# Decoder trunk with windowed attention: second key tile's rotation ahead of the second maxima, its split one pass later, early output weights' splits behind the second maxima

## The chip, the cores and the metric

The kernel runs as one program on one core of a Trainium2 chip. The metric is the device time of one execution in microseconds (us). All times inside the profiled execution are counted from the start of its span.

## The reference

The program is a two-layer decoder trunk in float32 for 512 tokens of width 1024: a gated short convolution with a SwiGLU layer, then sliding-window attention with sinks on shared keys and values, with another SwiGLU layer. The change touches only the attention, of which this is the core:

```python
k_sh = partial_rotary(k_sh.reshape(bsz, s, N_KV_HEADS, HEAD_DIM), cos, sin)
q = partial_rotary(q, cos, sin)
attn = sliding_window_sink_attention(q, k_sh, v_sh, b_sinks[j]) @ b_w_o[j]
# in sliding_window_sink_attention, 16 query heads on 4 key heads, blocks of 128, window 128:
scores = jnp.einsum('bnqhgd,bnkhd->bnhgqk', qb, kk).astype(jnp.float32) * scale
scores = jnp.where(valid[None, :, None, None], scores, NEG)
probs = jax.nn.softmax(jnp.concatenate([scores, sink], axis=-1), axis=-1)[..., :-1]
out = jnp.einsum('bnhgqk,bnkhd->bnqhgd', probs.astype(v.dtype), vv)
```

## The kernel before

Every float32 matrix operand is split into a high part (ACT copies it to a narrower type) and a low part (an elementwise engine subtracts), and each product is three matmuls: high by low, high by high, low by high. So for each operand there is an ACT instruction and a subtraction on DVE or POOL.

The attention runs in ten passes over eight pairs of heads, in the loop at the end of the kernel. Pass i works on several pairs at once: scores, maxima, exponents and scaling of pair i; transposition and the product with the values (`weigh`) of pair i-1; projection, rotation and split of the queries of later pairs. Each engine carries out its instructions in program order, and that order is written by hand in the string `ORDER` (line 47), one token a step, in which the digit is the half or the quarter of the step and a trailing `-` means one pair earlier. The tokens that matter here:

- `S0`, `S1`: `scores` (L1306, PE) of the two halves, into the two banks called psc. Both halves use the same two banks, so S1 waits until the maxima of the first half have read them, and S0 of the next pass waits for the maxima of the second half.
- `M0`, `M1`: `maxima` (L1318, DVE): four instructions, each adds the mask, scales and takes the row minimum of the negated scores. `E..`: `exponents` on ACT (L1334, L1341). `N0`, `N1`: `normalise` on DVE: a sum `se` (L1346), a reciprocal (L1348) and four scalings `s` (L1351).
- `T0` to `T3`: `turn` (L1363, PE): transposes the scaled exponents of the pass before. `P`, `L`: the split of what was transposed, `phi` on ACT (L1376) and `plo` on DVE (L1380; `lp` for the last block). `W0` to `W3`: `weigh`, the matmuls called po. `O-`: the split of po (L1400 ACT, L1401 DVE).
- `Q0` to `Q3`: projection of the queries (pq, L192 to L194, PE). `R-`: their rotation, `rope`: a shuffle (L1244) and a product with the cosines (L1246) on DVE, then a product with the sines (L1247) and a sum (L1248) on POOL. `H-`: `rope_split`: `rhl` on ACT (L1253) and on POOL (L1254).
- `K`: the same `rope` and `rope_split` for the second of two key tiles, in pass 2 alone. Its operand is the bank pk[1]; its results, `rhi` and `rlo`, are first read by S0 of pass 4. The first key tile was rotated before the loop.
- `G`: the split of query weights, `whi` on ACT (L187) and `wlo` on DVE (L188). `g0`, `g1`: the same for four tiles of the output weights ("early", used by `Z0`, `Z1` from pass 5 on), which happens in passes 4 and 6 (L187, L188 in pass 4, two half tiles by L181, L182 in pass 6). Their loads are issued by SP in the order of the program, through a ring of seven buffers.

POOL's queue also issues transfers that sum blocks of weights for the second SwiGLU layer in memory (`issue`, L546, tiles hsum), some behind each `R-` and each `H-`.

Of the kernel before, what the change touches and what calls it, by code (L numbers as in the profile page):

```python
# [44 lines left out]

EARLY_IN, REST_IN = 2, 0
ORDER = (
    "R- S0 T0 g0 T1 O- Q0 M0 Q1 Z0 P0 P1 S1 T2 T3 L0 Q2 L1 G M1 E00 E01 H- Q3 P2 P3 E10 E11 Z1 z0 K W0 L2 L3 A A A N0 W1 W2 N1 W3 g1 z1"
)
STEP = {  # L50
    "S": "scores", "M": "maxima", "E": "exponents", "N": "normalise", "T": "turn", "P": "high",
# [22 lines left out]
def yoco_kernel(  # L74
# [22 lines left out]
    nc = tc.nc  # L97
# [19 lines left out]
    def slot(s, dt=F32, w=S):  # L117
        return big.tile([P, w], dt, tag="slot", name=name(s), padded_shape=[P, S])
# [4 lines left out]
    def halves(s, dt=F32):  # L123
        w = wide(s, dt)
        return w[:, :S], w[:, S:]
# [3 lines left out]
    def bank(s, pool=None):  # L129

        if pool is None:
            pool = (ps_mm, ps_sc, ps_mm, ps_pt)[turn[0] % 4]
            turn[0] += 1
        return pool.tile([P, S], F32, tag="bank", name=name(s))
# [39 lines left out]
    def split_weights(src, raw=None, slots=False):  # L174
        if raw is None:
            raw = fetch(src)
        if slots:
            hi, lo = Two("whi", F32R), Two("wlo", F32R)
            for h in range(2):
                c = slice(h * S, (h + 1) * S)  # L180
                nc.scalar.activation(hi[:, c], raw[:, c], AF.Copy)  # L181
                nc.vector.tensor_tensor(out=lo[:, c], in0=raw[:, c], in1=hi[:, c].bitcast(F32),  # L182
                                        op=ALU.subtract)
            return hi, lo
        hi = wsp.tile([P, D], F32R, tag="whi", name=name("whi"))
        lo = wsp.tile([P, D], F32R, tag="wlo", name=name("wlo"))
        nc.scalar.activation(hi, raw, AF.Copy)  # L187
        nc.vector.tensor_tensor(out=lo, in0=raw, in1=hi.bitcast(F32), op=ALU.subtract)  # L188
        return hi, lo
# [347 lines left out]
    def issue(n, behind=None):  # L537

        for dst, src, op in issues[:n]:
            if len(dst.shape) == 3:  # L540
                dst, src = (t.rearrange("k (a b) c -> (k a) (b c)", b=4) for t in (dst, src))
            else:
                dst, src = (t.rearrange("(a b) c -> a (b c)", b=2) for t in (dst, src))
            kw = {} if op is None else {"accum_op": op}
            made = tc.keep_in_program_order(
                nc.gpsimd.dma_start(dst, src, max_dma_last_dim=4 * 4 * S, **kw))  # L546
            if behind is not None:
                tc.add_manual_dep(
                    made.ins, behind.ins.name, mybir.DependencyInfo(
                        mybir.DependencyClass.Sync, mybir.DependencyReason.DATA),  # L550
                    reason="pace")
        del issues[:n]
# [3 lines left out]
    for l in range(2):  # L556
# [3 lines left out]
        for rd, (f0, f1) in enumerate(ROUNDS[:-1]):  # L560
            k = slice(f0 // 2, f1 // 2)
# [4 lines left out]
    def sum_on(at):  # L566

        issue(len(issues))
        if at in BEGIN:
            summing.append(sums_of[BEGIN[at]])  # L570
        for x in summing:
            x.step()
        summing[:] = [x for x in summing if x.steps]
# [295 lines left out]
    def close(ws, x, k0, res, ahead, then=None, each=2):  # L869


        n = len(x) - k0

        def part(ps, t, half, ks):
            unit(ps, t, ws[len(ws) // 2 * half :], x, ks, n, k0)

        begun = [bank("pmix", ps_mm) for _ in range(2)]
        for half in range(2):
            part(begun[half], 0, half, range(n - 1))
            for _ in range(each if half == 0 or each > 1 else 0):  # L880
                ahead.one()
        for t in range(NB):
            for half in range(2):
                if t == 0:
                    ps = begun[half]
                    part(ps, t, half, range(n - 1, n))
                else:
                    ps = bank("pmix", ps_mm)
                    if (t, half) == (NB - 1, 1):
                        part(ps, t, half, range(2))  # L890
                        for b in range(4):
                            res.turn(b, (0, 1))
                        part(ps, t, half, range(2, n))
                        for f in range(4):
                            res.split(0, f, 0)
                        res.square_mix(t, 0)
                        res.square(NB - 2)
                        res.scale(t, 0)
                    else:
                        part(ps, t, half, range(n))  # L900
                res.take(t, half, ps)
                if (t, half) != (NB - 1, 0):
                    res.square_mix(t, half)
            if t < NB - 1:
                tile_done(res, t, square=t < NB - 2)
            if t == 0 and then:
                then()
# [40 lines left out]
    def first_weights(l):  # L948
        return ([w_gu[l, f, j] for f in range(2) for j in range(2)]
                + [w_gb[l, 0, b] for b in range(2)])  # L950
# [274 lines left out]
    pk = [bank("pk", ps_mm) for _ in range(2)]  # L1225
# [16 lines left out]
    def rope(ps, eng):  # L1242
        sh = slot("sh")
        nc.vector.stream_shuffle(sh, ps, swap)  # L1244
        a = slot("ra")
        nc.vector.tensor_tensor(out=a, in0=ps, in1=ctab, op=ALU.mult)  # L1246
        eng.tensor_tensor(out=sh, in0=sh, in1=stab, op=ALU.mult)  # L1247
        eng.tensor_tensor(out=a, in0=a, in1=sh, op=ALU.add)  # L1248
        return a

    def rope_split(a, eng, large=False):
        hi, lo = halves("rhl", F32R) if large else (slot("rhi", F32R), slot("rlo", F32R))
        nc.scalar.activation(hi, a, AF.Copy)  # L1253
        eng.tensor_tensor(out=lo, in0=a, in1=hi.bitcast(F32), op=ALU.subtract)  # L1254
        return hi, lo
# [172 lines left out]
    with tc.manual_schedule(engines=ALL):  # L1428
        last_tile(res, [[(0, 4)], [(0, 5)], [], [(0, 6), (0, 7), (1, 0), (1, 1)],
                        [(1, f) for f in (4, 5, 2, 3, 6, 7)]])  # L1430
        for hf in range(2):
            c = slice(hf * 256, (hf + 1) * 256)
# [32 lines left out]
        ks = [rope_split(rope(pk[0], nc.vector), nc.vector)]  # L1465
# [15 lines left out]
    with tc.manual_schedule(engines=ALL):  # L1481
        sum_on("a0")
        for i in range(KT + 2):
            if i == KT:
                res = Update(mix_o, B_ATT, [G_FPRE[1]])
                res.leaves = True
                ahead = Ahead(first_weights(1))
            if i == KT + 1:
                res.load()
            for c in ORDER.split():  # L1490
                if c == "A":
                    if i == KT:
                        ahead.one()
                    continue
                if c == "K":
                    if i == 2:
                        ks.append(rope_split(rope(pk[1], nc.gpsimd), nc.gpsimd))
                    continue
                late = c.endswith("-")
                op, n = c[0], [int(d) for d in c[1:].rstrip("-")]  # L1500
                t = i - late
                if op == "g":

                    u = 2 * (t - EARLY - 1) + n[0]
                    if u in (-2, -1, 2, 3):
                        j = u + 2 if u < 0 else u
                        early_w.append(split_weights(w_o[j // 2, j % 2], slots=j >= EARLY_IN))
                    continue
                if op in "SMENTPLWO":
                    t -= op in "TPLWO"  # L1510
                    of = hp
                elif op in "QRH":
                    t += LEAD
                    of = qs
                elif op == "G":
                    t += LEAD + 1
                    of = qs
                    if KT <= t < KT + 4:
                        j = t - KT
                        rest_w.append(split_weights(w_o[j // 2, 2 + j % 2], slots=j >= REST_IN))  # L1520
                else:
                    t = 2 * (t - EARLY - 1) + n.pop(0)
                    of = early
                if 0 <= t < len(of) and not (op in "RH" and t < LEAD - 1):
                    getattr(of[t], STEP[op])(*n)
                if op in "RH" and i <= KT:
                    issue(len(issues) // 2 if op == "R" else len(issues))
            if i <= KT:
                sum_on(f"a{i + 1}")
        close(rest_w, at, EARLY, res, ahead, lambda: sum_on(f"a{KT + 2}"), 1)  # L1530
# [96 lines left out]
```

## Time and profile before

| | |
|---|---|
| runs shown | 1022.95, 1023.82, 1023.06 us (median 1023.06) |
| the profiled execution | 1023.55 us |
| its span, first to last instruction | 1021.8 us |
| mean granted TensorE clock | 0.998 |
| the ten passes of the attention | about 549 to 655 us of the span |

A row of the timeline gives the start, the duration, the engine, the line of the kernel, the operation, output and inputs, shapes and, where the engine sat idle before it, how long and what ended that (in brackets). Rows of like instructions are merged (x2, x4). Pieces of the chain that ended last have start, duration, engine and tile. Matmuls overlap, so the distance between the starts of two of them says more than a duration. Pass 2 begins with S0 at 569.02, pass 3 at 581.39, pass 4 at 595.29 and pass 5 at 608.03 us.

### The profile page before, as it was taken

Reading aid. Unit: us, or ns where it says so; the run is one execution under the profiler, and the core shown is the slowest. Engines: PE = TensorE matmul, PEld = TensorE weight load, DVE = VectorE, ACT = ScalarE, POOL = GpSimd, SP = SyncE. Lnnn points to the kernel's source line nnn. Section 1 sums busy time; section 2 is a strip of 40 time slices with the busy share of each in tenths; the row PEclk is TensorE's granted clock in tenths of the full one; section 3 lists DMA queues with packets and bytes.
Section 4 is the critical chain, followed back from the end, with each engine's and each line's share of the span. In section 5 each row is a group of like instructions: output and inputs, shape, how many; then the busy total and the mean of one; then the engine's idle time right before and its main releaser. Section 6 shows DMA issues by size and latency. Waiting matters only on the chain.

```text
span 1021.8 us, 16273 instructions
## 1 busy us (share of the span) xinstructions
PE 1011.7 (99%) x6008; PEld 893.5 (87%) x6008; DVE 869.4 (85%) x1480; ACT 582.3 (57%) x1035; POOL 197.3 (19%) x259
## 2 busy tenths in 40 slices
PE   9999999999999999999999999999999999999997
PEld 8888888999889898998898788889998998989986
DVE  5766767899789999998869998778997899999896
ACT  6322444875655455566476676668666564645641
POOL 0443033112111111000123663231111010110001
PEclk9999999999999999999999999999999999999999
DMA  9897789549979699779404889976899676979742
GB/s 357 284 263 227 179 253 341 161 165 283 344 242 298 208 300 339 221 217 337 167 6 160 187 220 299 249 249 160 261 296 328 176 238 226 296 271 268 257 155 83
DMA packets 66575, 244.50 MB, mean 239 GB/s; under 512 B 7872, under 2 KB 8384, under 8 KB 54720
## 3 DMA queue, kind: packets, MB, share of 16 engines
q1 hardware_dynamic: 51328, 145.98, 38.7%
q0 software_dynamic: 14592, 96.48, 37.2%
q10 hardware_dynamic: 576, 1.02, 0.3%
q8 instruction: 47, 0.77, 0.3%
q14 instruction: 32, 0.26, 0.1%
HBM read 237.15 MB, written 102.76 MB: 333 GB/s over the span
## 4 chain that ended last, share of the span: by engine, by line
PE 90%; DVE 5%; ACT 2%; issue 1%; POOL 0%; DVEq 0%; ACTq 0%
PE gx L1055 14%; PE gx L1058 7%; PE pcub L193 4%; PE pcub L194 4%; PE pcub L192 4%; PE gz L194 4%; PE gz L192 4%; PE gz L193 4%; PE px L192 3%; PE px L193 3%; PE px L194 3%; PE pmix L193 2%; PE pmix L192 2%; PE pmix L194 2%; PE gy L193 2%; PE gy L192 2%
## 5 line engine op out<-in xcount | busy, mean ns | idle before, releaser
L478 DVE TENSOR_TENSOR wlo<-raw,whi 128x1024 fp32r<-128x1024 f32 x225 | 274.7, 1225 | 54.5 <-ACT whi L477 54.4
L477 ACT ACTIVATE whi<-raw 128x1024 fp32r<-128x1024 f32 x225 | 233.7, 1051 | 103.5 <-DVE raw L465 29.2
L1055 PE MATMUL gx<-xt,whi 128*128 128x512 f32 x480 | 120.4, 393 | 0.0
L1055 PEld LDWEIGHTS gx<-xt,whi 128*128 128x128 f32 x480 | 86.3, 189 | 15.5
L546 POOL DMA_DIRECT2D hsum<-in_w_gb_dram x96 | 62.9, 735 | 150.2 <-ACT whi L477 89.9
L546 POOL DMA_DIRECT2D hsum<-hsum x32 | 25.4, 792 | 291.0 <-ACT whi L477 219.4
L1017 DVE TENSOR_TENSOR st<-gx,st 128x256 f32<-128x256 f32 x200 | 77.9, 419 | 2.6 <-ACT st L1033 0.5
L1033 ACT ACTIVATE st<-gx 128x256 f32<-128x256 f32 x120 | 43.2, 380 | 62.3 <-PE gx L1058 58.7
L1058 PEld LDWEIGHTS gx<-xt,wlo 128*128 128x128 f32 x480 | 65.5, 190 | 4.7
L1058 PE MATMUL gx<-xt,wlo 128*128 128x256 f32 x480 | 66.9, 282 | 0.0
L1069 ACT ACTIVATE gr<-gr 128x1024 f32<-128x1024 f32 x20 | 21.2, 1062 | 50.2 <-DVE gr L1017 50.2
L192 PE MATMUL px<-wlo,ahi 128*128 128x512 f32 x120 | 46.8, 390 | 0.1
L194 PE MATMUL px<-whi,alo 128*128 128x512 f32 x120 | 46.7, 389 | 0.0
L193 PE MATMUL px<-whi,ahi 128*128 128x512 f32 x120 | 46.7, 389 | 0.0
L194 PE MATMUL gz<-xhi,wlo 128*128 128x256 f32 x160 | 45.5, 284 | 0.0
L192 PE MATMUL gy<-xlo,whi 128*128 128x256 f32 x160 | 45.3, 283 | 0.0
L193 PE MATMUL gy<-xhi,whi 128*128 128x256 f32 x160 | 45.3, 283 | 0.0
L192 PE MATMUL gz<-xt,whi 128*128 128x256 f32 x160 | 45.3, 283 | 0.0
L193 PE MATMUL gz<-xt,whi 128*128 128x256 f32 x160 | 45.3, 283 | 0.0
L194 PE MATMUL gy<-xhi,wlo 128*128 128x256 f32 x160 | 45.3, 283 | 0.0
L192 PE MATMUL gz<-xlo,whi 128*128 128x256 f32 x160 | 45.3, 283 | 0.0
L194 PE MATMUL gz<-xt,wlo 128*128 128x256 f32 x160 | 45.3, 283 | 0.0
(298 smaller groups left out, 2999.4 us busy)
## 6 DMA issues: line engine op xcount, KB each, us to landing
hsum<-in_w_gb_dram POOLq DMA_DIRECT2D x96, 512.0 KB, 7.8
raw<-hsum SPq DMA_DIRECT2D x88, 512.0 KB, 7.8
raw<-in_w_gb_dram SPq DMA_DIRECT2D x60, 512.0 KB, 6.7
hsum<-in_w_dn_dram POOLq DMA_DIRECT2D x36, 512.0 KB, 8.1
raw<-in_w_dn_dram SPq DMA_DIRECT2D x32, 512.0 KB, 6.5
hsum<-hsum POOLq DMA_DIRECT2D x28, 512.0 KB, 5.4
raw<-in_w_in_dram SPq DMA_DIRECT2D x21, 512.0 KB, 7.6
hsum<-in_w_dn_dram POOLq DMA_DIRECT2D x12, 768.0 KB, 12.5
```

Of the source, the lines that this page charges most:

```text
L192: nc.tensor.matmul(out, whi, xlo, start=start, stop=False, **kw)
L193: nc.tensor.matmul(out, whi, xhi, start=False, stop=False, **kw)
L194: nc.tensor.matmul(out, wlo, xhi, start=False, stop=stop, **kw)
L477: self.begun = nc.scalar.activation(hi[:, :n], raw, AF.Copy)
L478: nc.vector.tensor_tensor(out=lo[:, :n], in0=raw, in1=hi[:, :n].bitcast(F32), op=ALU.subtract)
L546: nc.gpsimd.dma_start(dst, src, max_dma_last_dim=4 * 4 * S, **kw))
L1017: nc.vector.tensor_tensor(out=out, in0=a, in1=b, op=ALU.add)
L1033: nc.scalar.activation(ste, a, AF.Copy)
L1055: nc.tensor.matmul(banks[c][e], whi[:, kk], factors[p][k][2], start=opened and k == 0, stop=False, **kw)
L1058: nc.tensor.matmul(banks[c][e][:, :256], wlo[:, kk], factors[p][k][0], start=False, stop=k == 3 and p == 4, **kw)
L1069: nc.scalar.activation(kept[2], kept[2], AF.Silu)
```

## The change

The string is written in another order, and the step `K` is cut in two: the rotation stays in pass 2 but stands ahead of `M1`, and the split, now called `k`, stands in pass 3 behind `H-`. `g0` moves from behind `T0` to a place behind `M1`, `H-` and `k`. The number of instructions and their shapes don't change.

```diff
-    "R- S0 T0 g0 T1 O- Q0 M0 Q1 Z0 P0 P1 S1 T2 T3 L0 Q2 L1 G M1 E00 E01 H- Q3 P2 P3 E10 E11 Z1 z0 K W0 L2 L3 A A A N0 W1 W2 N1 W3 g1 z1"
+    "R- S0 T0 T1 O- Q0 M0 Q1 Z0 P0 P1 S1 T2 T3 L0 Q2 L1 G K M1 E00 E01 H- k g0 Q3 P2 P3 E10 E11 Z1 z0 W0 L2 L3 A A A N0 W1 W2 N1 W3 g1 z1"
...
                 if c == "K":
                     if i == 2:
-                        ks.append(rope_split(rope(pk[1], nc.gpsimd), nc.gpsimd))
+                        rot_k = rope(pk[1], nc.gpsimd)
+                    continue
+                if c == "k":
+                    if i == 3:
+                        ks.append(rope_split(rot_k, nc.gpsimd))
                     continue
```

The order of PE's instructions is the same in both programs. On DVE, pass 2, around the second maxima (ISA, the last of four instruction pairs, here on the bank psc_5988), this stands before:

```order
L1318 ISA s_6027,nm_6025<-psc_5988,mask,nsnk 128x256
L1318 ISA nm_6025 128x1
L1244 STREAM_SHUFFLE sh_6061<-pk_5213 128x512
L1246 TENSOR_TENSOR ra_6063<-pk_5213,ctab_5216 128x512
L1380 TENSOR_TENSOR plo_6007<-pt_6001,phi_6006 128x512
```

And this stands there now, with the first of the four pairs at its end:

```order
L188 TENSOR_TENSOR wlo_6022<-raw_6019,whi_6021 128x1024
L1244 STREAM_SHUFFLE sh_6025<-pk_5213 128x512
L1246 TENSOR_TENSOR ra_6027<-pk_5213,ctab_5216 128x512
L1318 ISA s_6032,nm_6031<-psc_5987,mask,nsnk 128x256
L1318 ISA nm_6031 128x1
```

The key tile's shuffle and product have moved from behind the four maxima to ahead of them, so that `plo` of the third transposition now follows the maxima at once.

On POOL, passes 2 and 3, from the query rotation of pass 2 on (sh_5927), this stands before:

```order
L1248 TENSOR_TENSOR ra_5929<-ra_5929,sh_5927 128x512
L546 DMA hsum_178<-hsum_176 64x2048
L1254 TENSOR_TENSOR rhl_6040<-ra_5929,rhl_6040 128x512
L546 DMA hsum_180<-in_w_gb_dram 64x2048
L546 DMA hsum_181<-in_w_gb_dram 64x2048
L1247 TENSOR_TENSOR sh_6061<-sh_6061,stab_5217 128x512
L1248 TENSOR_TENSOR ra_6063<-ra_6063,sh_6061 128x512
L1254 TENSOR_TENSOR rlo_6068<-ra_6063,rhi_6067 128x512
L1247 TENSOR_TENSOR sh_6112<-sh_6112,stab_5217 128x512
```

Now the key tile's two rotation steps (sh_6025, ra_6027) come first, in two pieces of the queue, of which this is the one in pass 2:

```order
L546 DMA hsum_178<-hsum_176 64x2048
L1247 TENSOR_TENSOR sh_6025<-sh_6025,stab_5217 128x512
L1248 TENSOR_TENSOR ra_6027<-ra_6027,sh_6025 128x512
L1254 TENSOR_TENSOR rhl_6046<-ra_5929,rhl_6046 128x512
L546 DMA hsum_180<-in_w_gb_dram 64x2048
```

And this is the one at the end of pass 3, with the first step of pass 4 behind it:

```order
L1254 TENSOR_TENSOR rhl_6221<-ra_6110,rhl_6221 128x512
L546 DMA hsum_182<-in_w_gb_dram 64x2048
L546 DMA hsum_183<-in_w_gb_dram 64x2048
L1254 TENSOR_TENSOR rlo_6227<-ra_6027,rhi_6226 128x512
L1247 TENSOR_TENSOR sh_6287<-sh_6287,stab_5217 128x512
```

The rotation has moved ahead of the query split `rhl` of pass 2 and of two transfers, and the key split `rlo` stands behind the query split and two transfers of pass 3.

On DVE, pass 4, at its start, the split of an early output weight (wlo_6320) stood between the query rotation and the split of po:

```order
L1244 STREAM_SHUFFLE sh_6287<-pq_6150 128x512
L1246 TENSOR_TENSOR ra_6289<-pq_6150,ctab_5216 128x512
L188 TENSOR_TENSOR wlo_6320<-raw_6317,whi_6319 128x1024
L1401 TENSOR_TENSOR ohl_6330<-po_6246,ohl_6330 128x512
L1318 ISA s_6341,nm_6340<-psc_6296,mask,nsnk 128x128
```

Now it stands behind the second maxima (wlo_6411) and ahead of the third `plo`:

```order
L1318 ISA s_6389,nm_6387<-psc_6350,mask,nsnk 128x256
L1318 ISA nm_6387 128x1
L188 TENSOR_TENSOR wlo_6411<-raw_6408,whi_6410 128x1024
L1380 TENSOR_TENSOR plo_6369<-pt_6363,phi_6368 128x512
L1380 TENSOR_TENSOR lp_5548<-pt_6370,lp_5547 128x2x128
```

In pass 6 the two half tiles move in the same way. On ACT the copies move with their splits: `whi` of `g0` and `rhi` stand behind `rhl`, ahead of the third `phi`. SP issues the load of the query weights of pass 4 ahead of that of the early output weights of the same pass, where it was the other way round.

## The prediction

> **What bounds the kernel now.** The page comes first: the busy shares and the chain of work that ended last.
>
> ```profile
> PE 1011.7 (99%) x6008; PEld 893.5 (87%) x6008; DVE 869.4 (85%) x1480; ACT 582.3 (57%) x1035; POOL 197.3 (19%) x259
> ...
> PE 90%; DVE 5%; ACT 2%; issue 1%; POOL 0%; DVEq 0%; ACTq 0%
> ```
>
> PE sets the time nearly everywhere. A change that leaves PE's instructions alone can win only what PE waits, so I look for the stretch where the chain leaves PE. In the chain's pieces between 545 and 665 us, DVE stands there from 579 to 599 us, with nothing else between that is longer than half a us; these are its first piece, what stands ahead of it, and its last.
>
> ```profile
> 578.51 0.51 issue
> 579.02 0.69 DVE plo L1380
> ...
> 598.56 0.68 DVE ohl L1401
> ```
>
> So in passes 2 to 4 of the attention DVE is late and PE waits for it. How much, PE's timeline tells: S0 of passes 2, 3, 4 and 5 (569.02, 581.39, 595.29, 608.03), S1 of passes 2, 3 and 4 (573.71, 587.59, 600.32), and places with a gap.
>
> ```profile
> 569.02 0.39 PE L1306 MATMUL psc<-rlo,rhl 64*128 64x256 f32 x2
> 573.71 0.38 PE L1306 MATMUL psc<-rlo,rhl 64*128 64x256 f32 x2
> 579.37 0.28 PE L194 MATMUL po<-phi,vt 128*128 128x256 f32 x1
> 579.77 0.39 PE L192 MATMUL po<-plo,vt 128*128 128x256 f32 x1
> 579.99 0.28 PE L193 MATMUL po<-phi,vt 128*128 128x256 f32 x1
> 580.11 0.28 PE L194 MATMUL po<-phi,vt 128*128 128x256 f32 x1
> 581.39 0.39 PE L1306 MATMUL psc<-rlo,rhl 64*128 64x256 f32 x2
> 583.26 0.44 PE L1363 MATMUL pt<-ident,s 128*128 128x128 f32 x2 [0.42 <-DVE s L1351]
> 587.59 0.76 PE L1306 MATMUL psc<-rlo,rhl 64*128 64x256 f32 x2 [0.29 <-DVE nm L1318]
> 595.29 0.39 PE L1306 MATMUL psc<-rlo,rhl 64*128 64x256 f32 x2
> 600.32 0.76 PE L1306 MATMUL psc<-rlo,rhl 64*128 64x256 f32 x2 [0.28 <-DVE nm L1318]
> 608.03 0.39 PE L1306 MATMUL psc<-rlo,rhl 64*128 64x256 f32 x2
> ```
>
> Passes 2, 3 and 4 hold the same PE work, and take 12.37, 13.90 and 12.74 us from S0 to S0. Pass 2 has one hole: the po matmuls start 0.12 us apart (579.99 to 580.11), but 0.40 and 0.22 apart around 579.77, so 0.38 is lost. An undisturbed pass is then 12.37 - 0.38 = 11.99 us; pass 3 loses 13.90 - 11.99 = 1.91 and pass 4 loses 0.75. **Together 3.04 us is all that this change can reach**, 0.3% of the time.
>
> **The change, part by part.** First the rotation. These are DVE's rows of passes 2 to 4, in order: the second maxima, the key's two instructions, the third `plo`, then N0 and the start of N1, the rotation of pass 3, the two `plo` behind its first maxima, its N0, the rotation of pass 4 and two `wlo` of that pass.
>
> ```profile
> 574.82 0.48 DVE L1318 CUSTOM_DVE_ANT_0 s<-psc,mask,nsnk 128x256 f32<-128x256 f32 x1
> 576.45 0.74 DVE L1244 STREAM_SHUFFLE sh<-pk 128x512 f32<-128x512 f32 x1
> 577.09 0.67 DVE L1246 TENSOR_TENSOR ra<-pk,ctab 128x512 f32<-128x512 f32 x1
> 579.02 0.69 DVE L1380 TENSOR_TENSOR plo<-pt,phi 128x512 fp32r<-128x512 f32 x1 [1.26 <-ACT se L1341]
> 579.96 0.97 DVE L1346 TENSOR_TENSOR se<-se,rs 128x4 f32<-128x4 f32 x1
> 581.18 2.03 DVE L1351 TENSOR_SCALAR s<-s,rd 128x128 f32<-128x128 f32 x4
> 583.13 0.15 DVE L1346 TENSOR_TENSOR se<-se,rs 128x4 f32<-128x4 f32 x1
> 584.59 0.74 DVE L1244 STREAM_SHUFFLE sh<-pq 128x512 f32<-128x512 f32 x1
> 587.76 1.28 DVE L1380 TENSOR_TENSOR plo<-pt,phi 128x512 fp32r<-128x512 f32 x2
> 593.05 1.01 DVE L1351 TENSOR_SCALAR s<-s,rd 128x128 f32<-128x128 f32 x4
> 595.45 0.74 DVE L1244 STREAM_SHUFFLE sh<-pq 128x512 f32<-128x512 f32 x1
> 596.67 1.97 DVE L188 TENSOR_TENSOR wlo<-raw,whi 128x1024 fp32r<-128x1024 f32 x1
> 601.71 1.21 DVE L188 TENSOR_TENSOR wlo<-raw,whi 128x1024 fp32r<-128x1024 f32 x1
> ```
>
> The key's two DVE instructions cost 1.23 us (0.64 from start to start, 0.59 for the second) wherever they stand; moving them saves nothing by itself. What is lost behind them is (a) an idle 1.26 us ahead of `plo`, (b) 0.8 on `se` (0.97 against 0.15) and (c) 1.0 on the four scalings (2.03 against 1.01). For (a) the trace names ACT, which ended 0.5 us sooner (the "issue" piece at 578.51). By the waits built into the program, that `plo` takes a buffer which PE's first value products still read; in the changed program it takes one that POOL's rotation of the same pass gave up at 572.7, so (a) goes. For (b) and (c), POOL and ACT:
>
> ```profile
> 571.39 1.30 POOL L1248 TENSOR_TENSOR ra<-ra,sh 128x512 f32<-128x512 f32 x1
> 579.63 1.28 POOL L1248 TENSOR_TENSOR ra<-ra,sh 128x512 f32<-128x512 f32 x1
> 581.66 1.40 POOL L1254 TENSOR_TENSOR rlo<-ra,rhi 128x512 fp32r<-128x512 f32 x1 [0.74 <-ACT rhi L1253]
> 591.28 1.06 POOL L546 DMA_DIRECT2D hsum<-in_w_gb_dram  x2
> 597.63 2.15 POOL L1248 TENSOR_TENSOR ra<-ra,sh 128x512 f32<-128x512 f32 x1
> ...
> 592.60 0.47 ACT L1341 ACTIVATE se<-nm,snk 128x2 f32<-128x2 f32 x2
> ```
>
> The long `se` (579.96 to 580.93) ends with the key's POOL sum (579.63 to 580.91), the long scalings lie over `rlo` (581.66 to 583.06), and the 1.97 us `wlo` lies beside POOL's rotation, whose sum takes 2.15 instead of 1.30. The maxima keep their 0.48 beside POOL. The Trainium skill, "SBUF — State Buffer", section "Who interferes with whom", gives a reason: a DVE instruction with two SBUF inputs, or in a two-port mode, and a GpSimd instruction that reads SBUF exclude each other, and whichever starts first keeps the shared ports to its end. Those rows agree with it, and by it the pairing of POOL's instructions with `se`, scalings and `wlo` decides.
>
> Now the times, with the same distances from start to start. Maxima start 1.23 later, 576.05, and take 1.63 to 577.7; S1 of pass 2 is long done, and the next S0 wants its banks only at 581. `plo` and `lp` 0.94: 578.6. POOL starts the key's product at 575.6 behind the shuffle; at 1.3 us each, product, sum and the query split `rhl` end at 579.5. `se` at 578.6 waits for that to 579.6 (the cost of (b) stays); N0 is clean, since `rlo` is gone: 580.8. ACT's second exponents, which ended at 578.51, follow maxima that come 1.23 later, and end by 579.7, ahead of N1. So **N1's `se` comes at 580.9 instead of 583.13, 2.2 us sooner**. PE, without its 0.38, starts S0 at 581.0 (`rhl`, which it needs, is there 1.5 us before) and T0 at 581.9: the holes at 583 close. From N1's `se` to the last first-half maximum are 4.63 us (583.13 to 587.76): 585.5. PE arrives at S1 4.69 behind S0 (573.71 - 569.02): 585.7. That hole closes too, barely. Pass 3 loses nothing, and S0 of pass 4 comes at 581.0 + 11.99 = 593.0.
>
> In pass 3 the key split is new. ACT's `rhi` delays the third `phi` and the exponents by about 0.6, the time of any such copy; their sums, which ended at 593.0 (592.60), come 2.2 sooner and 0.6 later, 591.4, still ahead of N1. `rlo` lies behind the query split and two transfers, which ended at 592.3 (591.28) and come about 2 us sooner, so it runs from 590.3, over N0 again: the 1.0 us of (c) comes back here. From 585.5 to the rotation of pass 4 are 7.69 us (587.76 to 595.45), with that 8.7: 594.2. N0, over at 594.0 before, ends at 592.8, ahead of T0 at 593.9. `rlo` is done near 591.8, needed at 593.0.
>
> In pass 4, without the `wlo`, the first maxima end 3.2 us behind the rotation (584.59 to 587.76 in pass 3), at 597.4; S1 comes at 593.0 + 4.69 = 597.7. The 0.75 goes. Then `plo` twice, `wlo` and the second maxima, 4.0 us (587.76 to 591.72): 601.4. The moved `wlo` costs 1.2 clean, and 0.8 more if it meets POOL's `rhl` for its whole length (1.97 against 1.21); I take 0.3 of that, since `rhl` starts first: 602.9; `plo` ends at 603.5. PE's third value product is 10.5 behind S0 (579.37 + 0.12 - 569.02), 603.5, and a waiting matmul starts 0.14 behind `plo` (579.02 + 0.61 against 579.77): **a new hole of some 0.3 us** with its slow first step. This edit is bounded by nothing (no collision) and by 0.8 (a whole one); I take 0.3, nearer to the clean row. N0 ends at 605.1, ahead of T0 of pass 5 (605.9). Pass 5 is 5 us longer on PE, where DVE catches up. In pass 6 DVE waits for PE ahead of the second maxima:
>
> ```profile
> 631.26 0.48 DVE L1318 CUSTOM_DVE_ANT_0 s<-psc,mask,nsnk 128x256 f32<-128x256 f32 x1 [0.62 <-PE psc L1306]
> ```
>
> The two half `wlo` behind them, 1.2 together, and their copies on ACT then lie under the early output products of PE; without that cover they would cost up to 1.2. The swapped loads are issued several passes ahead of their use. The transfers on POOL that come 3 us later feed the next layer, for which PE shows no wait.
>
> **The sum**: -0.38 - 1.91 - 0.75 + 0.3 = -2.74. Against the profiled execution, 1023.55: 1020.8. The median of the runs shown is 0.49 lower, so I predict a median of **1020.3**.
>
> **The rivals.** *S1 keeps waiting.* My margins at S1 are 0.2 us in pass 3 and 0.3 in pass 4. If DVE comes half a us to 1 us later (wait (a) stays in some form, or a collision that I don't see), T0 and the value product still win, but S1 keeps waits like the 0.75 of pass 4 in both passes, and the rest of the gain, 1.3, is left, 1021.8, a result within 0.2%, which is about what a measurement of this kernel can tell from no change. For it: DVE runs without idle time from 579 to 604. Against: 2.2 us come free in one place.
>
> *`rlo` is held back by DVE.* If N0 and N1 of pass 3 keep POOL out until they end (594.2), `rlo` ends at 595.5, S0 of pass 4 stands 2.5 us, and the gain is 0.2: 1022.9. Against it: at 581.66 `rlo` took 1.40 against 1.30 while the scalings took 2.03, so POOL got in after one scaling. This is the skill's lock (same page and section), with DVE first; the trace so far shows POOL first.
>
> *`rlo` behind a transfer that waits: slower.* `rlo` now stands behind two transfers of POOL's queue. Later in the attention one of these kept POOL for long:
>
> ```profile
> 565.03 1.27 POOL L546 DMA_DIRECT2D hsum<-in_w_gb_dram  x2
> 653.49 0.80 POOL L546 DMA_DIRECT2D hsum<-in_w_gb_dram  x1 [10.47 <-DMA hsum<-in_w_gb_dram]
> DMA to landing us min/median/max: 4.5/8.4/16.2
> ```
>
> With such a wait in pass 3, `rlo` would end 10.5 us later, at 602 instead of 592, and S0 of pass 4 would lose 9: 1023.06 - 2.7 + 9 = 1029. The change turns slower once that wait is over 4 us. Against: the transfers whose place is reused were issued by 566 us (565.03), and with the slowest landing, 16.2, are done by 582.
>
> **How the numbers follow.** Forecast 0.60; S1 keeps waiting 0.22; `rlo` held back 0.11; slower 0.07. The range leaves out the slower case and the far half of the third: down to 1019.7 (all 3.04 from the median, and 0.3 for the scatter of a median of runs that lie 0.9 apart), up to 1022.5 (gain 0.6). A gain over 0.2% is a time under 1021.0: the forecast nearly whole and a part of the second case, 0.62. Within 0.2%: 0.30. Slower: 0.08.
>
> **What would show it.** In the changed profile: S0 of passes 3, 4 and 5 at about 581.0, 593.0 and 605.3; no idle time ahead of the third `plo` of pass 2; N1's `se` of pass 2 near 580.9; no hole at T0 and T1 of pass 3; S1 of passes 3 and 4 without a wait for `nm`; a small hole at the third value product of pass 4; `rlo` near 590 to 592, over N0. I am wrong if S0 of pass 4 waits for POOL, if holes of the same size turn up in passes 5 to 7, or if the gain at 605 us is lost again before the end.

## The result, and the profile after

| | before | after |
|---|---|---|
| median of the runs compared | 1023.30 us (7 runs, 1022.90 to 1023.82) | 1019.99 us (7 runs, 1019.85 to 1020.55) |
| profiled execution, and its span | 1023.55 us, 1021.8 us | 1020.08 us, 1018.3 us |
| mean granted TensorE clock | 0.998 | 0.999 |
| from S0 of pass 0 to S0 of pass 7 | 88.47 us | 85.42 us |
| passes 2, 3, 4, S0 to S0 | 12.37, 13.90, 12.74 us | 11.99, 11.99, 11.99 us |

The ratio is 0.9968, with a 95% interval of 0.9958 to 0.9978: 0.3% faster, 3.3 us in the medians, and the two sets of runs don't overlap. The busy shares and the shares of the chain, from the page of the changed kernel:

```profile
PE 1009.6 (99%) x6008; PEld 892.7 (88%) x6008; DVE 867.5 (85%) x1480; ACT 581.2 (57%) x1035; POOL 194.6 (19%) x259
PE 93%; DVE 3%; ACT 2%; issue 1%; DMA 0%; POOL 0%; DVEq 0%; SPq 0%; ACTq 0%
```

DVE's share of the chain fell from 5% to 3%, and PE's rose from 90% to 93%; the number of PE's instructions is unchanged. PE's timeline at the starts of the scores, S0 and S1 of passes 2, 3 and 4, and S0 of pass 5:

```profile
568.60 0.39 PE L1306 MATMUL psc<-rlo,rhl 64*128 64x256 f32 x2
573.28 0.39 PE L1306 MATMUL psc<-rlo,rhl 64*128 64x256 f32 x2
580.59 0.39 PE L1306 MATMUL psc<-rlo,rhl 64*128 64x256 f32 x2
585.27 0.38 PE L1306 MATMUL psc<-rlo,rhl 64*128 64x256 f32 x2
592.58 0.39 PE L1306 MATMUL psc<-rlo,rhl 64*128 64x256 f32 x2
597.27 0.38 PE L1306 MATMUL psc<-rlo,rhl 64*128 64x256 f32 x2
604.58 0.39 PE L1306 MATMUL psc<-rlo,rhl 64*128 64x256 f32 x2
```

No row has a wait in brackets any more. All three passes take 11.99 us and S0 to S1 4.68 or 4.69, so all of the 3.04 us that passes 2 to 4 could give came. The rest of the difference of the two spans (3.5) lies elsewhere: 0.4 of it is there at S0 of pass 2 already, ahead of everything that changed (568.60 against 569.02). When I compare an instant with the prediction below, I add these 0.42 to it.

DVE's timeline after, in order: third `plo`, `se` and scalings of N0, `se` of N1, all of pass 2; `se` of N0 in pass 3; the moved `wlo` and the third `plo` of pass 4.

```profile
577.09 0.69 DVE L1380 TENSOR_TENSOR plo<-pt,phi 128x512 fp32r<-128x512 f32 x1
578.02 1.02 DVE L1346 TENSOR_TENSOR se<-se,rs 128x4 f32<-128x4 f32 x1
579.29 1.05 DVE L1351 TENSOR_SCALAR s<-s,rd 128x128 f32<-128x128 f32 x4
580.26 0.15 DVE L1346 TENSOR_TENSOR se<-se,rs 128x4 f32<-128x4 f32 x1
...
589.78 1.05 DVE L1346 TENSOR_TENSOR se<-se,rs 128x4 f32<-128x4 f32 x1
...
600.59 1.22 DVE L188 TENSOR_TENSOR wlo<-raw,whi 128x1024 fp32r<-128x1024 f32 x1
601.73 0.68 DVE L1380 TENSOR_TENSOR plo<-pt,phi 128x512 fp32r<-128x512 f32 x1
```

And POOL's: the query split of pass 2, the key split of pass 3, the query split of pass 4.

```profile
577.71 1.31 POOL L1254 TENSOR_TENSOR rhl<-ra,rhl 128x512 fp32r<-128x512 f32 x1
...
589.49 1.31 POOL L1254 TENSOR_TENSOR rlo<-ra,rhi 128x512 fp32r<-128x512 f32 x1
...
598.94 1.44 POOL L1254 TENSOR_TENSOR rhl<-ra,rhl 128x512 fp32r<-128x512 f32 x1
```

The two long `se` end with POOL's instruction beside them (578.02 + 1.02 = 579.04 and 577.71 + 1.31 = 579.02; 590.83 and 590.80). On DVE, in passes 2 to 4, they are the whole price of the meetings that are left, 0.9 us each beyond the 0.15 of a clean `se`, and PE waits for neither.

### The profile page after: what moved, and what is told of

The parts are those of the page before. It is cut to its first block, busy times and chain, and to the rows that moved or that the text cites. A ratio compares the mean times of both kernels' runs of the same rounds, so it can differ in the third digit from the quotient of the medians.

```text
span 1018.3 us, 16274 instructions
## 1 busy us (share of the span) xinstructions
PE 1009.6 (99%) x6008; PEld 892.7 (88%) x6008; DVE 867.5 (85%) x1480; ACT 581.2 (57%) x1035; POOL 194.6 (19%) x259
## 3 DMA queue, kind: packets, MB, share of 16 engines
q10 hardware_dynamic: 576, 1.02, 0.3%
## 4 chain that ended last, share of the span: by engine, by line
PE 93%; DVE 3%; ACT 2%; issue 1%; DMA 0%; POOL 0%; DVEq 0%; SPq 0%; ACTq 0%
PE gx L1055 14%; PE gx L1058 7%; PE pcub L194 4%; PE pcub L192 4%; PE pcub L193 4%; PE gz L194 4%; PE gz L193 4%; PE gz L192 4%; PE px L192 3%; PE px L193 3%; PE px L194 3%; PE pmix L193 2%; PE pmix L192 2%; PE pmix L194 2%; PE gy L194 2%; PE gy L193 2%
```

## The experiments

Theory 1, the one behind the prediction: DVE works in program order and was late by three things in pass 2 (the idle time before the third `plo`, and POOL's key steps beside `se` and beside the scalings) and by one in pass 4 (the `wlo` of g0 beside POOL's rotation). Rival 2: the waits of pass 4 are only what is left over from pass 3, and g0's place doesn't matter. Rival 3: the split did it all, and the rotation's place doesn't matter. Because programs reach the attention at 548.2 to 549.3 us, I compare them by the passes of their profiles; the timed medians stand beside. All distances are from S0 to S0. A diff below shows only the tokens of `ORDER` around what moves (the whole string stands above), against the kernel that is named with it.

| kernel | pass 2 | pass 3 | pass 4 | passes 0 to 6, against before | median, and that of before beside it | ratio (95%) |
|---|---|---|---|---|---|---|
| before | 12.37 | 13.90 | 12.74 | 0 | | |
| after | 11.99 | 11.99 | 11.99 | -3.05 | 1019.99, 1023.30 | 0.9968 (0.9958 to 0.9978) |
| g0_only | 12.37 | 13.91 | 11.99 | -0.75 | 1022.88, 1023.07 | 0.9999 (0.9990 to 1.0007) |
| rot_split | 11.99 | 11.99 | 13.43 | -1.59 | 1022.05, 1023.07 | 0.9989 (0.9980 to 0.9998) |
| rot_only | 12.37 | 14.29 | 12.74 | +0.38 | 1023.90, 1023.07 | 1.0007 (0.9998 to 1.0016) |
| split_only | 11.99 | 12.79 | 13.65 | -0.59 | 1022.70, 1023.07 | 0.9996 (0.9987 to 1.0005) |
| split_g0 | 11.99 | 12.79 | 11.99 | -2.29 | 1020.86, 1023.28 | 0.9976 (0.9967 to 0.9986) |
| split_behind_L2 | 11.99 | 13.49 | 12.73 | -0.83 | 1022.35, 1023.28 | 0.9991 (0.9982 to 1.0000) |
| g0_first | 11.99 | 11.99 | 12.69 | -2.35 | 1020.75, 1023.28 | 0.9974 (0.9964 to 0.9983) |
| n0_pass7 | 11.99 | 11.99 | 11.99 | -3.04 | 1020.19, 1023.28 | 0.9967 (0.9955 to 0.9980) |
| near_split | 11.99 | 14.15 | 11.99 | -0.88 | 1022.34, 1023.53 | 0.9988 (0.9979 to 0.9997) |
| rot_rlo_dve | 13.38 | 12.06 | 12.71 | -0.86 | 1022.75, 1023.53 | 0.9997 (0.9987 to 1.0007) |
| near_split_dma_behind | 11.99 | 12.72 | 11.99 | -2.32 | 1021.11, 1023.19 | 0.9980 (0.9970 to 0.9989) |

### g0_only: g0's move alone

Against the kernel before:

```diff
-S0 T0 g0 T1
+S0 T0 T1
...
-H- Q3
+H- g0 Q3
```

> The kernel before with g0 alone moved behind H- (K whole at its old place in pass 2). Theory 1 (two chains: the key's steps make DVE late up to S1 of pass 3, g0's subtraction beside POOL's rotation makes it late at S1 of pass 4): passes 2 and 3 stay at 12.4 and 13.9 us, S0 to S1 of pass 4 falls from 5.03 to 4.7 and pass 4 from 12.74 to 12.0; gain 0.75 us (0.6 to 0.9). Rival 2 (the waits of pass 4 are only what is left of DVE's lateness from pass 3, and g0's place matters nothing): pass 4 stays near 12.7, gain 0 (below 0.2).

Measured: passes 2 and 3 as before, pass 4 11.99, S0 to S1 of pass 4 4.68; 0.75 us less within the passes. That is the theory's number, and rival 2 falls: DVE came as late out of pass 3 as before, and pass 4 still lost nothing. The times show only 0.2 less, within their scatter.

### rot_split: the change without g0's move

Against the changed kernel:

```diff
-S0 T0 T1
+S0 T0 g0 T1
...
-H- k g0 Q3
+H- k Q3
```

> The changed kernel with g0 back behind T0. Theory 1: passes 2 and 3 take 12.0 us each, 2.3 us gained by S0 of pass 4; but in pass 4 the subtraction of g0 lies beside POOL's rotation again, and the first maxima end 1.3 to 1.7 us after PE wants S1, so that pass 4 takes 13.3 to 13.7 us and only 1.35 to 1.65 us are left (1.5). Rival 2 (pass 4 waits only because DVE came late out of pass 3): passes 2, 3 and 4 take 12.0 us each and the whole gain of 3.0 us is there without g0's move.

PE's and DVE's timelines of pass 4 in this kernel (S0, S1, and the `wlo` of g0):

```profile
593.34 0.39 PE L1306 MATMUL psc<-rlo,rhl 64*128 64x256 f32 x2
599.07 0.35 PE L1306 MATMUL psc<-rlo,rhl 64*128 64x256 f32 x1 [0.98 <-DVE nm L1318]
```
```profile
595.40 1.98 DVE L188 TENSOR_TENSOR wlo<-raw,whi 128x1024 fp32r<-128x1024 f32 x1
```

`wlo` takes 1.98 us beside POOL's rotation, S1 waits for the first maxima, and pass 4 takes 13.43 us, as the theory said (13.3 to 13.7) and longer than the 12.74 of before: PE now arrives sooner at maxima that are no sooner. So 0.69 of the 2.29 us that the rotation and the split win in passes 2 and 3 is given back at the next place where DVE is late, and g0's move, worth 0.75 alone, is worth 1.46 on top of them.

### rot_only and split_only: the two halves of the key step apart

In rot_only the rotation stands ahead of M1 and the split is still in pass 2, ahead of L2; in split_only the rotation is where it was and the split comes a pass later. g0 is at its old place in both. Both diffs are against the kernel before, with `K` cut in two as in the change; first rot_only, with the split in pass 2:

```diff
-G M1
+G K M1
...
-z0 K W0
+z0 k W0
```

> The key's rotation ahead of M1, but its split still in pass 2 at the old place, g0 at its old place. Theory 1: pass 2 takes 12.0 us (no idle time before the third plo); the key's rlo lies over scalings of pass 2 and costs DVE 0.7 to 1.0 us, so that S1 of pass 3 waits some 0.7 us (pass 3 12.7); in pass 4 g0's subtraction makes S1 wait some 1.0 us (pass 4 13.0); gain 1.3 us (0.9 to 1.7). Rival 3 (what held DVE was the split: rlo over the scalings and ACT's wait of 2.45 us for POOL's sum; where the rotation stands matters nothing): gain 0 (below 0.4), pass 3 stays above 13.5.

And split_only, with the split in pass 3:

```diff
-H- Q3
+H- k Q3
```

> The key's rotation at its old place behind M1, its split a pass later behind H-, g0 at its old place. Theory 1: the idle 1.26 us before the third plo and the long se stay, pass 2 stays at 12.4 us; the scalings of N0 in pass 2 fall from 2.03 to 1.01 us, so that S1 of pass 3 waits 1.0 us less (pass 3 12.8); but rlo costs 1.0 us over N0 in pass 3 and S1 of pass 4 comes no sooner than before, at 600.3 (pass 4 13.8); gain 0.2 us (0 to 0.5). Rival 3 (the split alone held DVE): passes 2 and 3 near 12.0, gain 2 to 2.3 us by S0 of pass 4, at least 1.3 us at the end.

rot_only missed the theory's numbers: nothing is won, pass 3 is even 0.4 us longer, and rival 3's numbers for it came (gain below 0.4, pass 3 above 13.5). Its DVE from the third `plo` of pass 2 on, and POOL:

```profile
579.27 0.69 DVE L1380 TENSOR_TENSOR plo<-pt,phi 128x512 fp32r<-128x512 f32 x1 [1.39 <-ACT se L1341]
...
580.21 2.38 DVE L1346 TENSOR_TENSOR se<-se,rs 128x4 f32<-128x4 f32 x1
```
```profile
579.64 1.60 POOL L546 DMA_DIRECT2D hsum<-in_w_gb_dram  x2
580.71 1.85 POOL L1254 TENSOR_TENSOR rlo<-ra,rhi 128x512 fp32r<-128x512 f32 x1
```

The idle time before the third `plo` is still there (1.39), and `se` takes 2.38 us, up to the end of `rlo` (582.59 and 582.56). In split_only the same `plo` waits for nothing, though the rotation stands right ahead of it:

```profile
576.30 0.67 DVE L1246 TENSOR_TENSOR ra<-pk,ctab 128x512 f32<-128x512 f32 x1
576.89 0.68 DVE L1380 TENSOR_TENSOR plo<-pt,phi 128x512 fp32r<-128x512 f32 x1
```

So the idle time hangs on the split, not on the rotation. I explain it so: the split's two tiles, written ahead of L2, take the buffer that is free, and `plo` gets the next one, which PE still reads. No row tells which buffer a tile got, but PE's rows agree. The sixth value product of the pass is the last that reads the first `phi`; here it is in the kernel before, and then in rot_only:

```profile
578.65 0.28 PE L194 MATMUL po<-phi,vt 128*128 128x256 f32 x1
```
```profile
578.89 0.28 PE L194 MATMUL po<-phi,vt 128*128 128x256 f32 x1
```

By these records it ends at 578.93 and 579.17, and the late `plo` starts 0.09 and 0.10 us behind it (579.02 and 579.27). ACT, which the trace names, had ended 0.52 us ahead of `plo` in the one and 0.12 in the other.

In split_only pass 2 is 11.99, against the theory's 12.4; pass 3 (12.79 for 12.8), pass 4 (13.65 for 13.8) and the end (0.59 for up to 0.5) are near it. Rival 3 has pass 2 right and pass 3 and the end wrong: with the split alone pass 3 still loses 0.8. I formed the theory anew: **the split's place decides the third `plo`'s buffer; the rotation's place decides only which POOL instructions meet N0.** The next two kernels were made for it.

### split_g0: everything but the rotation's move

Against the changed kernel:

```diff
-G K M1
+G M1
...
-z0 W0
+z0 K W0
```

> The key's rotation at its old place behind M1; its split a pass later and g0 moved, as in the change. Revised theory (the split ahead of L2 takes the buffer that the third plo would have had, and its rlo lies over the scalings: this is pass 2 and most of pass 3; the rotation's place is worth only the collision of POOL's sum with N0; g0's place is worth pass 4): passes 2, 3 and 4 take 12.0, 12.8 and 12.0 us, from S0 of pass 0 to S0 of pass 7 2.2 us less than before (the whole change has 3.05 less). Rival (the rotation ahead of M1 carries the change): at most 1.0 us less, pass 3 above 13.3.

Measured as expected: 11.99, 12.79, 11.99, and 2.29 us less. The change without the rotation's move keeps three quarters of the gain. The rest is in these rows of POOL and DVE in pass 2:

```profile
576.88 1.86 POOL L1247 TENSOR_TENSOR sh<-sh,stab 128x512 f32<-128x512 f32 x1
578.82 1.29 POOL L1248 TENSOR_TENSOR ra<-ra,sh 128x512 f32<-128x512 f32 x1
```
```profile
579.01 1.89 DVE L1351 TENSOR_SCALAR s<-s,rd 128x128 f32<-128x128 f32 x4
```

The key's sum lies over the first scaling, and the four take 1.89 instead of 1.05 us; the 0.84 come back as the 0.80 of pass 3.

### split_behind_L2: the split in pass 2, behind the third `plo`

Against the kernel before:

```diff
-W0 L2 L3
+W0 L2 k L3
```

(with K for the rotation alone, at its old place, and g0 at its old place)

> The kernel before with the key's split moved within pass 2 only, from ahead of L2 to behind it; rotation and g0 at their old places. Buffer theory: no idle time before the third plo of pass 2 (1.26 before), the hole at the third value product is gone and pass 2 takes 12.0 us; rlo now falls on the start of N1, so pass 3 takes between 13.0 and 14.3 us, pass 4 stays near 12.7. Rival (that plo waits for ACT's second exponents, as the trace names them, or for POOL): the idle time and the 12.4 us of pass 2 stay.

The third `plo` on DVE, without idle time:

```profile
577.22 0.68 DVE L1380 TENSOR_TENSOR plo<-pt,phi 128x512 fp32r<-128x512 f32 x1
```

Pass 2 takes 11.99 us; pass 3 13.49 and pass 4 12.73 are in the expected bands. One step within the pass was enough. Up to there ACT, which the trace names, and POOL carry out the same steps as before at the same distances from S0, and this `plo` starts 0.8 us ahead of the end of ACT's last exponent (578.03); so neither is what held it in the kernel before. What is left, and what PE's rows above agree with, is a buffer that PE still reads.

### g0_first: the price of a meeting

Against the changed kernel:

```diff
-R- S0
+g0 R- S0
...
-H- k g0 Q3
+H- k Q3
```

> The changed kernel with g0 ahead of R-, so that its subtraction comes ahead of the maxima again, but before POOL's rotation begins. Collision theory: wlo takes its clean 1.22 us there, M0 of pass 4 ends 1.1 to 1.2 us later than in the changed kernel, S1 has some 0.4 us to spare and waits 0.75 us; pass 4 takes 12.7 us. Rival (the subtraction costs 1.97 us wherever it stands ahead of M0, or S1 has nothing to spare): pass 4 takes 13.2 to 13.8 us, as with g0 behind T0 (13.43).

The `wlo` and the shuffle behind it on DVE, and S1 on PE, in pass 4:

```profile
593.35 1.22 DVE L188 TENSOR_TENSOR wlo<-raw,whi 128x1024 fp32r<-128x1024 f32 x1
...
594.49 0.74 DVE L1244 STREAM_SHUFFLE sh<-pq 128x512 f32<-128x512 f32 x1
```
```profile
597.49 0.35 PE L1306 MATMUL psc<-rlo,rhl 64*128 64x256 f32 x1 [0.23 <-DVE nm L1318]
```

The same instruction takes 1.22 us with POOL idle and 1.98 beside the rotation, and the pass 12.69 against 13.43 (rot_split): the difference of 0.74 is the price of the meeting. The clean one delays what leads to the maxima by 1.09: the shuffle starts 1.98 us behind S0 of pass 4 (594.49 and 592.51), against 0.89 in the changed kernel (593.47 and 592.58). The pass loses 0.70, so S1 of pass 4 has some 0.39 us to spare in the changed kernel; the prediction said 0.3.

### n0_pass7: a version that fills the same wait elsewhere

In pass 7 the third `plo` of the changed kernel sits idle for 1.9 us, by what I took for the same kind of wait. This kernel puts N0 into it.

```diff
-            for c in ORDER.split():
+            order = ORDER.replace("L2 L3 A A A N0", "N0 L2 L3") if i == KT - 1 else ORDER
+            for c in order.split():
```

> The changed kernel with N0 ahead of L2 in pass 7 alone, where the third plo sits idle 1.9 us. Buffer theory (the wait is for a buffer that PE's value products read, so N0 fits into it): plo still starts at the same distance from S0 of pass 7 (9.76 us), N0 lies ahead of it, and the hole of 0.25 us at the first transposition of pass 8 is gone; 0.2 to 0.3 us less, too little for the times to show. Rival (plo waits for something that N0 delays, ACT or POOL): plo comes 1.3 us later and PE waits for it.

PE's eight transpositions at the start of pass 8, in the changed kernel and then here:

```profile
646.05 1.39 PE L1363 MATMUL pt<-ident,s 128*128 128x128 f32 x8
```
```profile
645.96 1.04 PE L1363 MATMUL pt<-ident,s 128*128 128x128 f32 x8
```

`plo` starts 9.78 us behind S0 (9.76 in the changed kernel), with 0.60 of idle time left of 1.92, and the hole among the transpositions is gone (0.35 less). So nothing that N0 delays holds this `plo`. The run doesn't tell PE from ACT, whose last exponent ends close ahead of it in the changed kernel (643.70, `plo` 643.76). The time, 1020.19, can't be told from the changed kernel's.

### near_split, rot_rlo_dve, near_split_dma_behind: the 2.38 us of `se`

Open was why `se` stood for 2.38 us in rot_only, when `rlo` needs 1.3, and whether the split has to go a pass later at all. near_split is the changed kernel with the split in pass 2 behind L2; rot_rlo_dve is rot_only with `rlo` on DVE. The first diff is against the changed kernel (`k` now in pass 2), the second against rot_only.

```diff
-H- k g0 Q3 P2 P3 E10 E11 Z1 z0 W0 L2 L3
+H- g0 Q3 P2 P3 E10 E11 Z1 z0 W0 L2 k L3
```

> The changed kernel with the key's split not a pass later but in pass 2 behind L2 (rotation ahead of M1 and g0 as in the change). Buffer theory: behind L2 the split no longer takes the third plo's buffer, so pass 2 takes 12.0 us; its rlo runs over the scalings of N1 in pass 2 and costs DVE 0.7 to 1.2 us, of which S1 of pass 3 has 0.4 to spare: pass 3 12.3 to 12.8, pass 4 12.0; 2.2 to 2.7 us less than before from S0 of pass 0 to S0 of pass 7. Rival (only the pass of delay frees DVE): pass 2 or 3 as in the kernel before, under 1.5 us less.

```diff
-                        ks.append(rope_split(rot_k, nc.gpsimd))
+                        ks.append(rope_split(rot_k, nc.vector))
```

> The kernel with the rotation ahead of M1 and the split and g0 at their old places, where se of pass 2 took 2.38 us; now the key's rlo is on DVE instead of POOL, ahead of the third plo. Lock theory (se waited because POOL's rlo had the ports): se takes 0.15 to 0.6 us, DVE reaches N1 1.0 to 1.6 us sooner although it carries 0.7 us more, pass 3 falls from 14.29 to 12.8 to 13.3 us. Rival (POOL's two transfers, issued at that time, held se): se still takes 0.5 us or more beyond the end of lp, until the second transfer is issued. In both the third plo or the rlo ahead of it still waits for the buffer, and pass 2 stays at 12.4 us.

near_split: pass 2 and pass 4 as expected, pass 3 14.15 instead of 12.3 to 12.8. With 0.88 us less, these are the rival's numbers; whether its reason holds, that only the pass of delay frees DVE, the rows decide. POOL in pass 2, and the first scaling of N0 on DVE:

```profile
579.36 1.59 POOL L546 DMA_DIRECT2D hsum<-in_w_gb_dram  x2
580.43 1.83 POOL L1254 TENSOR_TENSOR rlo<-ra,rhi 128x512 fp32r<-128x512 f32 x1
```
```profile
579.70 2.65 DVE L1351 TENSOR_SCALAR s<-s,rd 128x128 f32<-128x128 f32 x1
```

It is held from its start, while POOL still issues the transfers, to 582.35, when `rlo` is over (582.26). In rot_rlo_dve the two transfers of pass 2 are issued with no instruction of POOL ready behind them (POOL, then DVE):

```profile
578.81 1.58 POOL L546 DMA_DIRECT2D hsum<-in_w_gb_dram  x2
```
```profile
578.86 0.69 DVE L1254 TENSOR_TENSOR rlo<-ra,rhi 128x512 fp32r<-128x512 f32 x1 [1.82 <-PE po L192]
...
580.41 0.15 DVE L1346 TENSOR_TENSOR se<-se,rs 128x4 f32<-128x4 f32 x1
```

`rlo` on DVE runs through the first transfer in its 0.69 us, and `se`, which starts when the transfers are over (580.39), takes 0.15. (The row of `rlo` names PE for the idle time, but ACT's `rhi`, which it reads, ended at 578.83 too, so it is no evidence for the buffer.) The changed kernel has a scaling in that place: its two transfers of pass 2, again with nothing ready behind them, are these.

```profile
578.94 1.70 POOL L546 DMA_DIRECT2D hsum<-in_w_gb_dram  x2
```

N0's scalings there start at 579.29, lie within the issue and take 1.05 us, as clean ones do (1.01). So issuing transfers alone doesn't hold DVE. (My pass lengths for rot_rlo_dve missed: `rlo` pushes the third `plo` back, PE waits 1.1 us for it in pass 2, 13.38, and pass 3 is 12.06; the sum, 25.44, is 1.2 under that of rot_only.) What is left is an instruction of POOL that is ready while transfers are issued ahead of it. near_split_dma_behind, against near_split, takes them from there:

```diff
                 if c == "k":
                     if i == 2:
                         ks.append(rope_split(rot_k, nc.gpsimd))
+                        issue(len(issues))
                     continue
...
-                if op in "RH" and i <= KT:
+                if op in "RH" and i <= KT and not (op == "H" and i == 2):
```

> The kernel with the split in pass 2 behind L2 (rotation ahead of M1, g0 moved), in which the first scaling of N0 took 2.65 us; now the two transfers that POOL issues in pass 2 ahead of the key's rlo are issued behind it. Theory (an instruction of POOL that is ready behind transfers being issued keeps DVE out for their issue too): rlo runs right behind rhl, the first scaling ends with it after 1.0 to 1.2 us, the four of N0 take 1.9 us instead of 3.37, N1 comes 1.5 us sooner, and pass 3 takes 12.6 to 12.8 us instead of 14.15; passes 2 and 4 12.0. Rival (rlo alone holds DVE for that long, or the scaling waits for something else): N0 stays above 3 us and pass 3 above 13.8.

POOL in pass 2, and the four scalings of N0:

```profile
579.03 1.29 POOL L1254 TENSOR_TENSOR rlo<-ra,rhi 128x512 fp32r<-128x512 f32 x1
580.26 1.66 POOL L546 DMA_DIRECT2D hsum<-in_w_gb_dram  x2
```
```profile
579.24 1.94 DVE L1351 TENSOR_SCALAR s<-s,rd 128x128 f32<-128x128 f32 x4
```

The four scalings take 1.94 instead of 3.37 us, pass 3 12.72 instead of 14.15, as expected; the gain in the medians, each against its own runs of before, goes from 1.2 to 2.1 us. So the pass of delay is worth 2.16 us with the transfers ahead of `rlo` (14.15 against 11.99), and 0.73 without; the change's place, in pass 3, has two transfers ahead of `rlo` as well, but there they lie beside the maxima and `plo`, which keep their times. None of these versions beats the changed kernel.

## Why the prediction came out as it did

**What bounds the kernel** and **the reach of 3.04 us** held: 0.38, 1.91 and 0.75 came to the hundredth, and no hole of their kind turned up later.

**The signs in the profile.** S0 of passes 3, 4 and 5, said for 581.0, 593.0 and 605.3, came at 581.01, 593.00 and 605.00 (with the 0.42 added); N1's `se` of pass 2, said for 580.9, at 580.68; the idle time, the holes at T0 and T1 and the waits of S1 went; `rlo` ran from 589.91 to 591.22.

**The step that failed** is the term of +0.3 in the sum, "a new hole of some 0.3 us" at the third value product of pass 4. There is none; these are the two matmuls there, the second being the one that reads `plo`:

```profile
602.93 0.28 PE L194 MATMUL po<-phi,vt 128*128 128x256 f32 x1
603.05 0.28 PE L192 MATMUL po<-plo,vt 128*128 128x256 f32 x1
```

`plo` was over at 602.41 (601.73 + 0.68), 0.6 us ahead of the second of them; I had forecast both for the same instant, 603.5. Two numbers were off. I took 0.3 for a meeting of the moved `wlo` with `rhl`; `rhl` was over at 600.38, before `wlo` began at 600.59, and the price was zero, the lower bound that I named. And I let the new `rlo` cost the scalings 1.0 us in pass 3; it met `se` alone and cost 0.9, and DVE reached pass 4 some 0.3 sooner. That is the difference between 2.74 and 3.04 us. That the median misses by the same 0.3 (1019.99 for 1020.3) is in part luck: the forecast counts from a median of 1023.06, and the runs of before that were compared have 1023.30, so the medians fell by 3.31, which is 0.26 more than the passes gave.

**A reason that was right in its effect and put in the wrong place.** I told the idle time (a) among the things that stand behind the rotation. The mechanism, a buffer that PE still reads, fits every run (split_behind_L2 above all), but it belongs to the split: rot_only keeps it, split_only loses it. For the change as it was made, with both moved, this makes no difference to the time; anyone who had taken the rotation's half alone on that reading would have lost 0.4 us in the passes.

**(b) and (c)** held as meetings of POOL with DVE. The Trainium skill ("SBUF — State Buffer", section "Who interferes with whom") has the loser blocked for the whole of the other's instruction; the 1.02, 1.05 and 1.98 us agree. It also says that the one that issues first keeps the ports. By the records, the scaling of near_split began at 579.70 and `rlo` at 580.43, and DVE was blocked all the same; here the trace differs from the rule, unless POOL's instruction claims the ports before its record starts, which no row shows. With DVE first, POOL stood: in pass 3 of the changed kernel `rhl` began at 587.00 beside a `wlo` that ended at 587.31, and took 1.47 us instead of 1.31.

**The rivals.** *S1 keeps waiting* would have come with half a us more on DVE: g0_first puts the margin of pass 4 at 0.39. *`rlo` held back by DVE*: `rlo` took its 1.31 us, and it was `se` that stood. *`rlo` behind a transfer that waits*: it started right behind the two transfers.

## What to carry to other kernels

When an engine sits idle for a "free" buffer, ask which tiles were written just ahead of it in program order: moving such a write by one step removed the wait, and the engine that the trace named had nothing to do with it. Parts of a change that free the same in-order engine at successive places don't add up one by one (0.75 and 1.59 alone, 3.05 together): each part alone is partly lost at the next late place, so judge them together. And where one engine blocks another through a shared resource, what decides is the pairing, so follow the moved instruction on both queues.

## What the runs showed of the hardware that I had not expected

An instruction of POOL that is ready behind transfers which POOL is issuing kept DVE out from the issue on, and not only for its own 1.3 us. This was seen twice: `se` took 2.38 us in rot_only, against 1.02 in the changed kernel, beside an instruction with no transfer ahead of it; a scaling took 2.65 us in near_split, against 1.16 with the transfers behind `rlo`. Transfers with nothing ready behind them held nothing (the four scalings of the changed kernel, 1.05 us). What in POOL's queue does this stays open.

The time outside the span differs between programs that are nearly the same: time less span is 1.77 us in the runs of before, 1.78 after, but 2.15 in rot_split, and 2.13 in rot_rlo_dve and near_split_dma_behind (medians). With the scatter of the start of the attention (548.2 to 549.3) it limits what a timing can say of parts of this size; the cause was not tried.
